# A two-layer encoder on one core: query units inside a gate's steps, unions ahead of weight sums, more low halves on GpSimd

## The chip, the cores and the metric

The kernel runs on one core of a Trainium2 chip, in one launch. The metric is the device time of one execution in microseconds (us), as the median of several runs. The core's engines are TensorE (PE in the profile; its weight loads are PEld), VectorE (DVE), ScalarE (ACT), GpSimd (POOL) and SyncE (SP, which here only issues transfers). Each runs its own list of instructions in the order in which the program wrote them, and waits for semaphores that the others raise.

## The reference, cut to what matters

Two layers, 512 tokens, 1024 channels. The change leaves every product as it is; what it moves belongs to the latent queries of branch A and to the gated feed-forward network.

```python
for l in range(DEPTH):
    h = rms_norm(x, attn_norm_g[l])
    c_q, c_kv, k_rope, gq, gk, gv, pool_in, gate_logits = split_columns(h @ w_in[l], IN_SIZES)
    o_mla = mla_branch(c_q, ...)      # q = rms_norm(c_q) @ w_uq: latent queries
    o_gqa = gqa_branch(gq, gk, gv, ...)
    o_pool = pool_branch(pool_in, ...)
    gates = sigmoid(gate_logits)
    merged = sum(gates[:, :, i] * (o_i @ w_branch_i[l]) for i in range(3))
    x = x + merged @ w_out[l]
    hf = rms_norm(x, ffn_norm_g[l])
    u = depthwise_conv(hf @ ffn_w_up[l], ffn_conv_w[l], ffn_conv_b[l])
    x = x + (silu(u[..., :D_FF]) * u[..., D_FF:]) @ ffn_w_down[l]
```

## The kernel before, in words

**Numbers and products.** All matrix products are float32 products in a reduced form (fp32r). Each operand is cut in two: a high half, which ScalarE rounds (`wh` of a weight, `HH`, `ah`, `qa`), and a low half, which is the rest (`wl`, `HL`, `al`, `qb`) and is a subtraction on VectorE or GpSimd. A product is three matmuls: high by high, low by high, high by low (`mm3`, line 491 through `mm`).

**Weights** come as one stream of pieces up to 512 columns wide, in the order of use. Pieces are packed into `raw` tiles up to 1024 wide, each filled by one transfer of SP; three such tiles rotate. `wnext` hands out the next piece and makes the halves of some pieces ahead: ScalarE writes `wh`, then `pick` chooses VectorE or GpSimd for `wl` by the planner's view of when each is free, unless `pool_only` is set, which puts them on GpSimd. Six `wh` and six `wl` buffers rotate.

**Pieces of seven.** Parts of the feed-forward products take seven block products for what needs eight (`products`, line 1911). For those a piece needs sums of its four blocks as well (`w_seven`): ScalarE copies one block into a PSUM tile (`ps_mi` or `ps_S`), VectorE makes the sums there (`both`, `third`, `fourth`), ScalarE rounds them (`hi`), VectorE makes their low half (`lo`). The plain blocks' low half (384 wide) is `rest`.

**The order** is not that of the source. `Clock` plans: every step of VectorE, ScalarE and GpSimd is put on a heap with a planned time and an assumed duration, and TensorE's own instructions advance the planned time; a step is written into its engine's list when the planned time passes it. `chain` runs steps one after the other, each after the planned end of the one before. Nothing of this is left at run time but the order of each engine's list and the semaphores.

**A layer's stages.** Input projections; grouped-query attention (GQA) with the gates and branch products of branch C as filling between its steps; latent attention (MLA) with the other branches as filling; the output product; the feed-forward network in two halves (`HALVES`: blocks 0 to 9, then 10 to 21). Each half first makes its up-products (`UPS`), then the down-products: for each of four pairs of output blocks (`m` = 0, 2, 4, 6) five or six calls of `products`, which fill four PSUM banks out of the six of the ring `acc`, `ST`, `AV` (two each), and then `unite`, which adds the four banks into the residual `XM`. The next pair starts on the two banks left and needs a third after 12 of its matmuls.

**In `unite`** ScalarE copies half of bank `b1` to `u`; VectorE adds `b0` to `XM` (and frees that bank), adds the other half of `b1` to the copy (and frees that bank), adds `b2` twice (and frees it), adds `u` to `b3`, and GpSimd and VectorE add the rest. In the first half `again` brings back `hsp` and `tsp`, which are cut into `HH`/`HL` and `tf` for the second half, low halves on GpSimd.

**Latent queries.** `make_q` makes one group's queries in four units of six matmuls, each into an `acc` bank that is free again when the unit's copy (`MQ`) is made. While such a unit list is active, one unit is put in on every even step of the gate that follows it; so the first unit stands ahead of the gate's first step, and its two weight pieces stand ahead of the gate's two.

Of the kernel before, what the change touches and what calls it, by code (L numbers as in the profile page):

```python
# [18 lines left out]
P = 128  # L19
T = 512  # L20
# [42 lines left out]
REST = 0.4  # L63
GAP = 2.0
PREP = (2, 5, 8, 11)
# [33 lines left out]
def _widths():  # L99

    r = [384] * KC + [T] * 8 + [T] * KC + [288] * 4 + [T] + [288] * 4
    for br in (2, 1, 0):
        late = []
        for k, _ in _order(br):
            if k in "nv":
                late = WIDTHS[k]
            else:
                r += WIDTHS[k][:1] + late + WIDTHS[k][1:]
                late = []
    return r + [T] * (2 * KC) + [T] * (4 * FC) + [T] * (2 * FC)  # L110
# [47 lines left out]
class Clock:  # L158
# [5 lines left out]
    def __init__(self):  # L164
        self.now, self.n, self.heap, self.busy = 0.0, 0, [], False
        self.fin, self.free, self.ready = 0.0, {}, {}
        self.source = self.last = None
        self.gives_way = {}
        self.locked = (0.0, 0.0)
# [50 lines left out]
    def chain(self, *steps, after=0.2):  # L220

        def go(n, source=None, since=None):
# [4 lines left out]
            if late and max(late) > self.now:  # L227
                self.at(max(late) - self.now, lambda: go(n))
                return
            eng, most = self.gives_way.get(fn, (None, 0.0))  # L230
# [83 lines left out]
def trunk(ctx: ExitStack, tc: tile.TileContext, x, w, prm, gb, cst, pad, out):  # L314
# [99 lines left out]
    def w_seven():  # L414
# [20 lines left out]
        def rest():  # L435
            e = pick(W_BIAS)
            e.tensor_tensor(los[0][:, :384], r[:, :384], f(his[0][:, :384]), ALU.subtract)
            done("wa", j)
            if j + 1 == len(pieces) or pieces[j + 1][0] > sl:
                at(max(0.0, ck.free[e.kind] - ck.now) + D_FREE, lambda: w_upto(sl + 1 + RAW))  # L440
# [14 lines left out]
        def lo():  # L455
            V.tensor_tensor(los[1], s[0], f(his[1]), ALU.subtract)
            done("w", j)

        chain(([("sums", j * L // len(pieces))] + ([("w", j - 2)] if seven[j - 2] else []), first), rest, after=0.0)
        chain(([("a21", j)], both), third, fourth, hi, lambda: done("wh", j), lo, after=0.01)  # L460
# [201 lines left out]
    def layer(l, sq, xsrc):  # L662
# [206 lines left out]
        def set_keys():  # L869
            for _, kb in KAB:  # L870
                G.memset(f(kb[64:P, :T]), 0.0)
                G.memset(f(kb[64:65 if "gqa" in PLAN else 96, :T]), 1.0)

        at(0.5, set_keys)

# [131 lines left out]
        def gates(br, okey, odst, mode):  # L1007
# [50 lines left out]
            for k, m in _order(br):  # L1058
                if k in mla_make:
                    extra, tick, when = mla_make[k](m), 0, k  # L1060
                    continue
                work = branch(m) if k == "b" else gate(m)
                more, first = True, tick
                while more:
                    n = tick - first
                    if extra and (tick % 2 == 0 if when == "q" else k == "g" and n in ((2, 6) if when == "n" else (3,))):
                        if next(extra, END) is END:
                            extra = None
                        yield
                    tick += 1  # L1070
                    more = next(work, END) is not END
                    yield
# [720 lines left out]
        def up_evac(c, part, acc, tag, scaled):  # L1793
# [77 lines left out]
            def turns():  # L1871
                eng = V if c + 1 == FC else G
                w0 = whole.pop(p)
                chain(diff(t3, 1, w0[:, 256:T], ALU.add), diff(t4, 0, t2, ALU.subtract), qfree,
                      *split(new[4][:, :T], new[5][:, :T], t34[:, :T], eng=eng), end(2), after=0.0)
                chain(*split(new[2][:, :T], new[3][:, :T], t12[:, :T], eng=eng), end(1), after=0.0)
# [10 lines left out]

        def products(right_, banks_, first, late=False):
            j = st["use"]
            his, los = (lambda z: (z[:2], z[2:]))(wnext())  # L1890
            (bh, bl), (ah, al), (ch, cl), (dh, dl), kb, ka, kc_, kd = right_
# [80 lines left out]
        def unite(m, banks_, then, early=False):  # L1972
# [10 lines left out]

            chain(lambda: A.activation(p1, b1[:, :256], AF.Copy), after=0.0)
            if early:
                chain(add(x0, x0, b0), add(u2, p1, b1[:, hi_]), add(x0[:, hi_], x0[:, hi_], b2[:, hi_]), add(x0, x0, u[:, :T]),
                      add(x1, x1, b2), add(b3[:, :256], u2, b3[:, :256]),
                      lambda: V.tensor_tensor(pair(x1), pair(x1), b3[:, None, :256].to_broadcast([P, 2, 256]), ALU.add), after=0.0)
                return
            chain(add(x0, x0, b0), lambda: free(t0), add(u2, p1, b1[:, hi_]), lambda: free(t1),  # L1990
                  add(x0[:, hi_], x0[:, hi_], b2[:, hi_]), add(x1, x1, b2), lambda: free(t2),
                  add(b3[:, :256], u2, b3[:, :256]),
                  add(x0, x0, u[:, :T], G), lambda: then and then(m),
# [28 lines left out]
        for c0, c1 in HALVES:  # L2022
            room[:] = spare
            for n_, (c, part) in enumerate(_ups(c0, c1)):
                if not c0 and n_ in PREP:
# [14 lines left out]
            for m in range(0, KC, 2):  # L2040
# [4 lines left out]
                for k in range(c0, c1 - 2 * PLAIN * end_, 2):  # L2045
                    products(right_of(k // 2), banks_, k == c0, m == 0 and k == c1 - 2)
                unite(m, banks_, finish if c1 == FC else None, end_)
# [80 lines left out]
def _pack_weights(i):  # L2128
    res = []
    for l in range(L):  # L2130
# [17 lines left out]
        for br in (2, 1, 0):  # L2148
            for k, m in _order(br):
# [7 lines left out]
                elif k == "q":  # L2157
                    res += [uq[kc * P:kc * P + P, m * 384:m * 384 + 384] for kc in range(2)]
                else:
# [98 lines left out]
```

## Time and profile before

| what | value |
|---|---|
| time, median of 3 runs | 1538.01 us (1537.58 to 1538.58) |
| the profiled execution's own time | 1538.08 us |
| its span | 1536.3 us |
| VectorE busy | 1206.2 us (79%) |
| ScalarE busy | 974.5 us (63%) |
| GpSimd busy | 1120.1 us (73%) |

In the profile a row of a timeline is: start, length, engine, line, operation, output tile <- input tiles, shape, how often in a row, and in brackets the idle time of the engine before it with what ended it. Matmuls overlap in time, so the length of a matmul row is longer than the step from its start to the next start. To see what a wait costs TensorE, take the distance of two starts and subtract the usual step.

### The profile page before, as it was taken

What the parts mean: (1) busy time and instruction counts of PE and PEld (TensorE: products, weight loads), DVE (VectorE), ACT (ScalarE), POOL (GpSimd) and SP (SyncE); (2) the same over time, 40 slices, a digit from 0 to 9 for tenths busy, and PEclk for the clock granted to TensorE, in tenths of its full rate; (3) what the DMA queues carried; (4) which work ended last, traced back from release to release, by engine and by line L of the source; (5) the groups of instructions that cost most, each with busy time, mean ns of one, the idle gap of its engine ahead of it and who ended that gap; (6) DMA issues with size and microseconds to landing.
All of it is one profiled execution on the core that took longest, in us unless ns stands there. A gap on an engine that the chain in (4) does not pass through costs nothing.

```text
span 1536.3 us, 25158 instructions
## 1 busy us (share of the span) xinstructions
PE 1519.1 (99%) x8390; PEld 1325.6 (86%) x8390; DVE 1206.2 (79%) x2386; ACT 974.5 (63%) x1961; POOL 1120.1 (73%) x1077
## 2 busy tenths in 40 slices
PE   9999999999999999999999999999999999999999
PEld 8888788788889899999998877888888899989998
DVE  6778889986578896778857788899865788867786
ACT  6557776664567665666654587766636677656763
POOL 4865986854689787675779659868547897967753
PEclk9999999999999999999999999999999999999999
DMA  6432234424344453333444322344243444533332
GB/s 219 117 111 78 76 92 139 130 91 132 105 140 147 148 176 106 94 103 109 133 129 136 102 70 76 112 134 130 79 151 96 141 148 138 182 107 100 95 121 84
DMA packets 91954, 183.56 MB, mean 119 GB/s; under 512 B 21936, under 2 KB 43696, under 8 KB 91824
## 3 DMA queue, kind: packets, MB, share of 16 engines
q1 hardware_dynamic: 91680, 181.94, 38.0%
q8 instruction: 66, 1.08, 0.3%
q14 instruction: 64, 0.52, 0.1%
q10 hardware_dynamic: 144, 0.01, 0.0%
HBM read 159.89 MB, written 22.02 MB: 118 GB/s over the span
## 4 chain that ended last, share of the span: by engine, by line
PE 75%; DVE 12%; ACT 6%; POOL 3%; issue 3%; DMA 1%; SPq 0%; ACTq 0%; DVEq 0%; POOLq 0%
PE ps_acc L491 24%; PE ps_AV L491 16%; PE ps_ST L1911 8%; PE ps_ST L491 8%; PE ps_acc L1911 7%; PE ps_AV L1911 6%; PE ps_S L491 2%; PE ps_mi L491 2%; ACT wh L272 2%; DVE nmt L290 1%; DVE wl L280 1%; DVE vt L284 1%; DVE XM L280 1%; DVE pl L280 1%; POOL qa L280 1%
## 5 line engine op out<-in xcount | busy, mean ns | idle before, releaser
L280 POOL TENSOR_TENSOR wl<-raw,wh 128x512 fp32r<-128x512 f32 (+3 forms) x487 | 579.7, 1200 | 306.3 <-ACT wh L272 267.0
L272 ACT ACTIVATE wh<-raw 128x512 fp32r<-128x512 f32 (+2 forms) x521 | 290.9, 577 | 21.1 <-PE ps_ST L491 11.3
L491 PE MATMUL ps_acc<-HH,wh 128*128 128x512 f32 x504 | 196.9, 391 | 0.1
L491 PE MATMUL ps_acc<-HL,wh 128*128 128x512 f32 x504 | 196.5, 390 | 0.0
L491 PE MATMUL ps_acc<-HH,wl 128*128 128x512 f32 x504 | 196.3, 389 | 0.0
L491 PEld LDWEIGHTS ps_acc<-HH,wl 128*128 128x128 f32 x504 | 94.6, 188 | 19.9
L491 PEld LDWEIGHTS ps_acc<-HH,wh 128*128 128x128 f32 x504 | 94.7, 188 | 19.7 <-DVE gt L280 0.6
L491 PEld LDWEIGHTS ps_acc<-HL,wh 128*128 128x128 f32 x504 | 94.7, 188 | 18.9
L491 PE MATMUL ps_AV<-HH,wh 128*128 128x512 f32 x248 | 96.7, 390 | 0.0
L491 PE MATMUL ps_AV<-HL,wh 128*128 128x512 f32 x248 | 96.6, 390 | 0.0
L491 PE MATMUL ps_AV<-HH,wl 128*128 128x512 f32 x248 | 96.5, 389 | 0.0
L272 ACT ACTIVATE wh<-ps_S 128x512 fp32r<-128x512 f32 x79 | 47.3, 598 | 49.2 <-DVE ps_S L280 37.8
L272 ACT ACTIVATE wh<-ps_mi 128x512 fp32r<-128x512 f32 x79 | 47.3, 598 | 46.5 <-DVE ps_mi L280 38.1
L280 DVE TENSOR_TENSOR wl<-ps_mi,wh 128x512 fp32r<-128x512 f32 x79 | 54.0, 684 | 12.2 <-ACT wh L272 10.6
L280 POOL TENSOR_TENSOR a<-a,cv 128x511 f32<-128x511 f32 x36 | 46.8, 1314 | 21.9 <-DVE a L284 21.9
L280 DVE TENSOR_TENSOR wl<-ps_S,wh 128x512 fp32r<-128x512 f32 x79 | 54.0, 684 | 10.6 <-ACT wh L272 9.7
L272 ACT ACTIVATE gt<-gt 128x512 f32<-128x512 f32 x48 | 30.2, 628 | 43.3 <-DVE gt L280 43.1
L1911 PE MATMUL ps_acc<-ah,wh 128*128 128x256 f32 x276 | 56.5, 283 | 0.0
L1911 PE MATMUL ps_ST<-ah,wh 128*128 128x256 f32 x294 | 55.5, 284 | 0.3 <-ACT wh L272 0.2
L290 DVE TENSOR_REDUCE nm<-ps_S 128x1 f32<-128x512 f32 x64 | 43.6, 682 | 15.1 <-PE ps_S L491 14.6
L272 ACT ACTIVATE ps_ST<-ps_ST 128x512 f32<-128x512 f32 x74 | 42.3, 583 | 20.1 <-PE ps_ST L491 12.4
L491 PEld LDWEIGHTS ps_AV<-HH,wl 128*128 128x128 f32 x248 | 46.6, 188 | 9.8
(560 smaller groups left out, 5201.2 us busy)
## 6 DMA issues: line engine op xcount, KB each, us to landing
raw<-w SPq DMA_DIRECT2D x228, 512.0 KB, 3.6
raw<-w SPq DMA_DIRECT2D x13, 384.0 KB, 3.1
XM<-x SPq DMA_DIRECT2D x16, 256.0 KB, 3.6
back<-hsp SPq DMA_DIRECT2D x16, 256.0 KB, 3.9
back<-tsp SPq DMA_DIRECT2D x16, 256.0 KB, 4.3
dtq<-tr SPq DMA_DIRECT2D x16, 192.0 KB, 1.9
dtk<-tr SPq DMA_DIRECT2D x16, 192.0 KB, 2.0
tf<-dtq SPq DMA_DIRECT2D x48, 64.0 KB, 2.1
```

Source lines behind the costliest of these rows:

```text
L272: return self.eng.activation(out, in_, func, **k)
L280: return self.eng.tensor_tensor(out, *a)
L284: return self.eng.scalar_tensor_tensor(out, *a)
L290: return self.eng.tensor_reduce(out, in_, *a, **k)
L491: PE.matmul(o, lhsT=lhsT, rhs=rhs, start=start, stop=stop)
L1911: PE.matmul(banks_[b][1][:, 256 * at_:256 * at_ + 256], lhsT=(his, his, los)[q][i][:, ws], rhs=right[n][q == 1], start=first and b not in ...
```

## The change

The edits are all of order and of the engine that does a step; the arithmetic is the same but for the place where the copy of `b1` is added.

- **Query units** (`_widths`, `_pack_weights`, `gates`): the two weight pieces of a query group now stand between the following gate's two pieces, and the units go in on odd steps, so the gate's first step comes first.
- **Union** (`unite`): ScalarE copies all 512 columns of `b1` and that bank is free; GpSimd, not VectorE, adds the two halves of the copy; VectorE's later step waits for that sum by the key `u2`.
- **Hold** (`HOLD`, `waits`, `pause`): `hi` and `lo` of a piece of seven, if planned between 0.65 us before and 0.15 us after the planned end of a pair's last products, are planned for the end of that stretch.
- **Low halves** (`ONLY`): in the first half of the feed-forward network `pool_only` is set, for `rest` of a piece of seven too.
- **Last turn**: in the second half the low half of `t34` of the last block goes to GpSimd as all others do.
- **GAP** 2.0 to 3.0: the cutting of what `again` brings is planned later.
- **set_keys**: four memsets of a layer go from GpSimd to VectorE, and are planned at 4.0 in place of 0.5.

```diff
-GAP = 2.0
+GAP = 3.0
+ONLY = True
+HOLD = (0.65, 0.15)
...
-            if k in "nv":
+            if k in "qnv":
                 late = WIDTHS[k]
             else:
                 r += WIDTHS[k][:1] + late + WIDTHS[k][1:]
...
-        self.gives_way = {}
+        self.gives_way, self.waits, self.pause = {}, set(), (0.0, 0.0)
...
+            if fn in self.waits and self.pause[0] <= self.now < self.pause[1] - 0.001:
+                self.at(self.pause[1] - self.now, lambda: go(n, source, since))
+                return
...
         def rest():
-            e = pick(W_BIAS)
+            e = G if pool_only[0] else pick(W_BIAS)
...
+        ck.waits.update((hi, lo))
...
         def set_keys():
             for _, kb in KAB:
-                G.memset(f(kb[64:P, :T]), 0.0)
-                G.memset(f(kb[64:65 if "gqa" in PLAN else 96, :T]), 1.0)
-
-        at(0.5, set_keys)
+                V.memset(f(kb[64:P, :T]), 0.0)
+                V.memset(f(kb[64:65 if "gqa" in PLAN else 96, :T]), 1.0)
+
+        at(4.0, set_keys)
...
-                    if extra and (tick % 2 == 0 if when == "q" else k == "g" and n in ((2, 6) if when == "n" else (3,))):
+                    if extra and (tick % 2 == 1 if when == "q" else k == "g" and n in ((2, 6) if when == "n" else (3,))):
...
-                      *split(new[4][:, :T], new[5][:, :T], t34[:, :T], eng=eng), end(2), after=0.0)
+                      *split(new[4][:, :T], new[5][:, :T], t34[:, :T], eng=G), end(2), after=0.0)
...
-        def products(right_, banks_, first, late=False):
+        def products(right_, banks_, first, late=False, end=False):
             j = st["use"]
+            if end:
+                ck.pause = (ck.now + 2.52 - HOLD[0], ck.now + 2.52 + HOLD[1])
...
-            chain(lambda: A.activation(p1, b1[:, :256], AF.Copy), after=0.0)
             if early:
+                chain(lambda: A.activation(p1, b1[:, :256], AF.Copy), after=0.0)
...
-            chain(add(x0, x0, b0), lambda: free(t0), add(u2, p1, b1[:, hi_]), lambda: free(t1),
+            chain(lambda: A.activation(u[:, :T], b1, AF.Copy), lambda: free(t1), add(u2, p1, u2, G), lambda k=c0: done("u2", l, m, k), after=0.0)
+            chain(add(x0, x0, b0), lambda: free(t0),
                   add(x0[:, hi_], x0[:, hi_], b2[:, hi_]), add(x1, x1, b2), lambda: free(t2),
-                  add(b3[:, :256], u2, b3[:, :256]),
+                  ([("u2", l, m, c0)], add(b3[:, :256], u2, b3[:, :256])),
...
+            pool_only[0] = ONLY and not c0
...
-                    products(right_of(k // 2), banks_, k == c0, m == 0 and k == c1 - 2)
+                    products(right_of(k // 2), banks_, k == c0, m == 0 and k == c1 - 2, k == c1 - 2)
...
                 elif k == "q":
-                    res += [uq[kc * P:kc * P + P, m * 384:m * 384 + 384] for kc in range(2)]
+                    late = [uq[kc * P:kc * P + P, m * 384:m * 384 + 384] for kc in range(2)]
```

Three places show how the lists of the engines change. First VectorE, at the union of the second pair in the first half of layer 0. `ps_mi` and `ps_S` are the tiles of weight sums, `wl` are low halves, `XM<-XM,ps_...` are the union's sums. Before:

```order
L280 TENSOR_TENSOR ps_mi_4839<-ps_mi_4839,raw_6321 128x256
L280 TENSOR_TENSOR wl_0_6447<-raw_6321,wh_0_6445 128x384
L280 TENSOR_TENSOR ps_mi_4839<-raw_6321,ps_mi_4839 128x128 x2
L280 TENSOR_TENSOR XM<-XM,ps_AV_6295 128x512
L280 TENSOR_TENSOR wl_1_6448<-ps_mi_4839,wh_1_6446 128x512
L280 TENSOR_TENSOR u_884_6480<-u_884_6480,ps_AV_6300 128x256
L280 TENSOR_TENSOR ps_S_4840<-ps_S_4840,raw_6321 128x256
L280 TENSOR_TENSOR XM<-XM,ps_acc_6314 128x256
```

After:

```order
L285 TENSOR_TENSOR ps_mi_4839<-ps_mi_4839,raw_6320 128x256
L285 TENSOR_TENSOR ps_mi_4839<-raw_6320,ps_mi_4839 128x128 x2
L285 TENSOR_TENSOR XM<-XM,ps_AV_6292 128x512
L285 TENSOR_TENSOR XM<-XM,ps_ST_6314 128x256
L285 TENSOR_TENSOR ps_S_4840<-ps_S_4840,raw_6320 128x256
L285 TENSOR_TENSOR XM<-XM,ps_ST_6314 128x512
L285 TENSOR_TENSOR ps_S_4840<-raw_6320,ps_S_4840 128x128
L285 TENSOR_TENSOR wl_1_6445<-ps_mi_4839,wh_1_6443 128x512
```

The low half of 384 columns is gone from VectorE's list, the sum into `u` too, and the weight sums' low half stands behind three of the union's sums.

GpSimd at the same place. `back` is what `again` brought, `tf` and `HL` its low halves, `XM<-XM,u` the union's part on GpSimd. Before:

```order
L280 TENSOR_TENSOR tf_6276<-back_6283,tf_6275 128x512
L280 TENSOR_TENSOR tf_6278<-back_6285,tf_6277 128x512
L280 TENSOR_TENSOR wl_0_6495<-raw_6321,wh_0_6493 128x384
L280 TENSOR_TENSOR wl_0_6536<-raw_6389,wh_0_6534 128x384
L280 TENSOR_TENSOR XM<-XM,u_884_6480 128x512
L280 TENSOR_TENSOR HL<-back_6485,HH 128x512
```

After:

```order
L285 TENSOR_TENSOR tf_6273<-back_6280,tf_6272 128x512
L285 TENSOR_TENSOR wl_0_6444<-raw_6320,wh_0_6442 128x384
L285 TENSOR_TENSOR u_884_6477<-u_884_6477 128x256
L285 TENSOR_TENSOR wl_0_6492<-raw_6320,wh_0_6490 128x384
L285 TENSOR_TENSOR tf_6275<-back_6282,tf_6274 128x512
L285 TENSOR_TENSOR XM<-XM,u_884_6477 128x512
L285 TENSOR_TENSOR wl_0_6537<-raw_6397,wh_0_6535 128x384
L285 TENSOR_TENSOR HL<-back_6482,HH 128x512
```

GpSimd has the 384 columns and the sum of `u` in addition, and the second `tf` stands behind them.

Third, GpSimd in the GQA stage of layer 0, where the other half of a pair's `qa` is made (`t_pair`, heads 4 and 5). `yt` and `y` are steps of the reciprocal root for the latent queries. Before:

```order
L280 TENSOR_TENSOR wl_1790<-raw_1541,wh_1789 128x512
L280 TENSOR_TENSOR yt_1723<-y_242_1722,ssm_1031 128x32
L280 TENSOR_TENSOR yt_1723<-yt_1723,y_242_1722 128x32
L294 TENSOR_SCALAR yt_1723<-yt_1723 128x32
L280 TENSOR_TENSOR y_242_1722<-yt_1723,y_242_1722 128x32
L280 TENSOR_TENSOR qa_1749<-tf_1585,qa_1749 64x512
```

After:

```order
L285 TENSOR_TENSOR wl_1723<-raw_1498,wh_1722 128x256
L285 TENSOR_TENSOR qa_1716<-tf_1583,qa_1716 64x512
L285 TENSOR_TENSOR qa_1719<-tf_1583,qa_1719 64x512
L315 MEMSET osum_1591 1x512 x2
L285 TENSOR_TENSOR oraw_1590<-oraw_1590,osum_1591 128x512
```

The four steps of the root now come later than `qa`, since the query units that feed them come later. Outside the two GQA stages TensorE's own list is the same in both but for the names of PSUM banks; in them, the query units stand at other places.

## The prediction

> **What bounds the kernel now.** I read the page first, then the list of who waited for whom on TensorE, then the timeline around each of its longer waits.
>
> ```profile
> span 1536.3 us, 25158 instructions
> PE 1519.1 (99%) x8390; PEld 1325.6 (86%) x8390; DVE 1206.2 (79%) x2386; ACT 974.5 (63%) x1961; POOL 1120.1 (73%) x1077
> ```
>
> TensorE is busy all the time and the change removes no matmul. So the whole prize is the time in which TensorE waits, and everything that the other engines save elsewhere is worth nothing. The page's 17 us of idle understate it, since matmul rows overlap; but the list tells for whom it waits:
>
> ```profile
> PE ps_AV L1911 <- DVE XM L280: 2.5, 2, 1.3
> PE ps_S L491 <- POOL qa L280: 2.0, 2, 1.0
> PE ps_ST L491 <- POOL qb L280: 1.4, 4, 0.4
> ...
> PE ps_ST L1911 <- DVE XM L280: 1.0, 2, 0.6
> ...
> PE ps_ST L1911 <- DVE wl L280: 0.6, 2, 0.4
> ```
>
> Nearly all come in twos: one a layer. Line 1911 is the feed-forward products, line 491 here the attention stage.
>
> **The first half's union.** The longest pair, 2.5 us, is where a new pair of blocks needs its third bank:
>
> ```profile
> 556.09 3.93 DVE L280 TENSOR_TENSOR wl<-raw,wh 128x384 fp32r<-128x384 f32 x1
> 560.47 0.68 DVE L280 TENSOR_TENSOR XM<-XM,ps_AV 128x512 f32<-128x512 f32 x1
> 557.05 2.55 POOL L280 TENSOR_TENSOR tf<-back,tf 128x512 fp32r<-128x512 f32 x2
> 559.42 0.40 PE L1911 MATMUL ps_acc<-sMK,wh 128*128 128x256 f32 x2
> 559.66 0.28 PE L1911 MATMUL ps_acc<-sMK,wl 128*128 128x256 f32 x1
> 561.20 0.51 PE L1911 MATMUL ps_AV<-sMQ,wh 128*128 128x256 f32 x2 [1.26 <-DVE XM L280]
> 561.90 0.28 PE L1911 MATMUL ps_AV<-sMK,wl 128*128 128x256 f32 x1
> 562.37 0.39 PE L1911 MATMUL ps_AV<-sMQ,wh 128*128 128x256 f32 x1 [0.20 <-DVE u L280]
> L272 ACT ACTIVATE wh<-ps_S 128x512 fp32r<-128x512 f32 x79 | 47.3, 598 | 49.2 <-DVE ps_S L280 37.8
> ```
>
> Two matmuls from 559.42 to 559.66 take 0.24, so one of 256 columns takes 0.12. From 559.66 to the next start at 561.20 are 1.54: 1.42 lost; 561.90 to 562.37 loses 0.35 more: 1.77 in all. The list's 2.5 for two waits, 1.3 the longest, says that layer 1 loses as much. The cause is one VectorE row: a low half of 384 columns, both inputs in SBUF, that runs from 556.09 to 560.02 while GpSimd works to 559.60. Behind it in VectorE's list stand the union's sums, which free the banks. The change puts this low half on GpSimd (in the first half all of them go there; three a layer move), and lets ScalarE free a bank by its own copy. Price of the new way: the third bank is wanted 12 x 0.12 = 1.44 after the new pair begins; a ScalarE copy of 512 columns from PSUM takes 0.60 (the fence's last row, from the page's groups) and VectorE's sum 0.68, side by side, so either is in time. I take the whole loss as gained: **-3.5** for two layers (-1.8 if half of it comes back).
>
> The Trainium skill, "SBUF — State Buffer", section "Who interferes with whom", says that a VectorE instruction with two SBUF inputs and a GpSimd instruction that reads SBUF shut each other out for a whole instruction. The trace agrees: the row ends 0.42 after GpSimd's run does. By that rule the new sum on GpSimd cannot be blocked by the union's sums on VectorE, which read PSUM; it changes no term.
>
> **The second half's begin and first union.**
>
> ```profile
> 719.94 0.28 PE L1911 MATMUL ps_ST<-ah,wl 128*128 128x256 f32 x1
> 720.44 0.50 PE L1911 MATMUL ps_ST<-ah,wh 128*128 128x256 f32 x2 [0.22 <-ACT wh L272]
> 721.16 0.39 PE L1911 MATMUL ps_ST<-ah,wl 128*128 128x256 f32 x1 [0.22 <-DVE wl L280]
> 724.14 0.28 PE L1911 MATMUL ps_acc<-sMK,wl 128*128 128x256 f32 x1
> 724.79 0.51 PE L1911 MATMUL ps_ST<-sMQ,wh 128*128 128x256 f32 x2 [0.37 <-DVE XM L280]
> 716.59 0.68 DVE L280 TENSOR_TENSOR ah<-ps_acc,ah 128x512 fp32r<-128x512 f32 x1
> 717.19 0.68 DVE L280 TENSOR_TENSOR ah<-t,ah 128x512 fp32r<-128x512 f32 x1
> 723.45 0.69 DVE L280 TENSOR_TENSOR wl<-ps_mi,wh 128x512 fp32r<-128x512 f32 x1 [0.74 <-ACT wh L272]
> 724.06 0.68 DVE L280 TENSOR_TENSOR XM<-XM,ps_ST 128x512 f32<-128x512 f32 x1
> ```
>
> At 720 weight sums come late: 0.50 - 0.12 = 0.38, then 0.72 - 0.24 = 0.48 lost. VectorE has three low halves of `ah` ahead of them; one moves to GpSimd, worth one step of 0.60 (716.59 to 717.19). So 0.6 of the 0.86 goes, in each layer: **-1.2** (0 to -2.2: layer 1 waits longer by the list). At 724, 0.65 - 0.12 = 0.53 and 0.10 behind it: the union's sum stands behind a weight's low half, begun 0.61 earlier. The hold turns the two round: 0.61 sooner, and ScalarE's copy frees a bank besides. The low half that now waits belongs to a product 2.52 (21 x 0.12) later, which hides it. By the list layer 1 loses 0.6 where layer 0 loses 0.37, so 0.9: **-1.5** (-0.7 to -1.5).
>
> **Attention.**
>
> ```profile
> 154.00 0.26 POOL L280 TENSOR_TENSOR yt<-y,ssm 128x32 f32<-128x32 f32 x1
> 155.31 1.81 POOL L280 TENSOR_TENSOR qa<-tf,qa 64x512 fp32r<-64x512 f32 x1
> 155.57 0.40 PE L491 MATMUL ps_acc<-HL,wh 128*128 128x512 f32 x1
> 155.80 0.39 PE L491 MATMUL ps_acc<-HH,wl 128*128 128x512 f32 x1
> 157.17 0.50 PE L491 MATMUL ps_S<-ka,qa 128*128 128x512 f32 x1 [0.98 <-POOL qa L280]
> 136.43 0.40 PE L491 MATMUL ps_acc<-HH,wl 128*128 128x512 f32 x1
> 137.50 0.44 PE L491 MATMUL ps_acc<-wh,cth 128*128 128x384 f32 x1 [0.67 <-DVE MQ L298]
> 95.54 0.33 PE L491 MATMUL ps_acc<-wh,cth 128*128 128x384 f32 x1
> 95.77 0.69 DVE L284 SCALAR_TENSOR_TENSOR XM<-gt,ps_acc 128x512 f32<-128x512 f32 x1
> ```
>
> A matmul of 512 columns takes 0.23. From 155.80 to 157.17 TensorE loses 1.14 on `qa`, and as the list has two such waits, 1.0 the longest, 1.14 in layer 1. GpSimd's `qa` stood behind four steps of a root (154.00 to 155.31: 1.31). These now stand behind it, as the query units that feed them come later; 1.31 sooner is more than 1.14: **-2.3** (-1.1 to -2.5: `qa` still follows a low half that waits for ScalarE). The second group's second query unit lost 1.07 - 0.23 = 0.84 in layer 0 for its bank, whose copy VectorE makes: six matmuls lay between (1.4). In the new list it is 13 (3.0): **-0.8** (0 to -0.8).
>
> Against that, the first query unit now takes the bank of the branch product just ahead, only three matmuls (0.68) after its last, where before a gate took it after six of 384 columns. The branch's product on VectorE ends at 96.46, TensorE would be there at 95.54 + 0.68 = 96.22, and resumes some 0.1 later: 0.3 a layer, **+0.6** (0 to +1.4). The other waits of this stage, above all the 1.4 for `qb`, are dealt anew with the order. Nothing in the rows says better or worse; GpSimd has more ahead of `qb` in places and less in others. I take **+1.0** (-2 to +4).
>
> **GpSimd's new work** in the first half's down-products:
>
> ```profile
> 546.00:586.00 40.00, 38.55 (x318) 38.05 (x317) 34.23 (x74) 25.84 (x61) 36.68 (x32) 1.00 0.52 172
> 562.23 1.99 POOL L280 TENSOR_TENSOR wl<-raw,wh 128x384 fp32r<-128x384 f32 x2 [2.62 <-ACT wh L272]
> 539.85 1.31 POOL L280 TENSOR_TENSOR ah<-t,ah 128x512 fp32r<-128x512 f32 x1 [0.93 <-ACT ah L272]
> L280 POOL TENSOR_TENSOR t<-a 128x256 f32<-128x256 f32 x22 | 16.4, 744 | 2.0 <-DVE a L280 2.0
> ```
>
> GpSimd is busy 36.68 of 40 there, and its one long gap (2.62) was the same VectorE row's doing. It gets three sums of `u` at 0.74, one low half of 384 columns at 1.0 (562.23: two in 1.99) and one of 512 at 1.3 (557.05: two in 2.55): 4.5, so 41.2 in 40 - 1.8 = 38.2. It falls 3.0 behind by the end of the stretch. Low halves are made two products ahead, 5.0, which covers it if it starts level (the 539.85 row). I take **+1.0** for two layers (0 to +6.0, the whole lag). The union's sum that needs `u` waits for GpSimd with VectorE's whole list behind it; VectorE has about 2.8 of other steps ahead of it (three sums at 0.6, one at 0.33 and two weight sums), against 0.74 and a low half of 1.0 on GpSimd, so it is covered at the first three unions.
>
> No cost for the rest: `kb`'s memsets and the replanned cuts lie where the list of waits shows none, the other twelve unions ended without a wait, the weights' bytes are the same, and in the second half GpSimd has room for the 0.74 and the 1.3 (724 to 769: no wait on it in the list).
>
> **Sum:** -3.5 - 1.2 - 1.5 - 2.3 - 0.8 + 0.6 + 1.0 + 1.0 = -6.7. The profiled execution took 1538.08 (the span and 1.8 around it), the median is 1538.01, so both give **1531.4**, 0.4% faster.
>
> **Rivals.** *Attention gives it back* (20%): the order planned with the same assumed durations has as many waits as before, each elsewhere. For it: the waits there ended on engines that ran late against the plan, and the plan's durations are unchanged. Then -2.3 and -0.8 are gone, and +0.6, +1.0 and +1.0 remain: 1538.1 - 6.2 + 2.6 = 1534.5. *No gain at the banks* (8%): another row of VectorE or a late ScalarE copy holds the unions, so the change does not do what it says. Then -3.5 and -1.5 fall out: 1536.4. Against it: the 3.93 row has no other cause in reach. *GpSimd becomes the bound in the first halves* (15%; slower than before): u's sum stands behind two more steps than I counted (a `tf` of 1.3 and a low half of 1.0), VectorE stands still at each of the eight unions there, and the next weight sums come late. A price of 1.3 a union (2.3 less about 1.0 of room) makes +10.4 in place of +1.0 and takes the -3.5: 1531.4 + 9.4 + 3.5 = 1544.3. It decides once GpSimd is over 3 us late at the first union. Against it: before, GpSimd is level with its work at 539.85, where it has waited 0.93 for ScalarE.
>
> The Trainium skill, "Perfetto Trace Analysis", section "Optimizing GPSIMD Operations", says to prefer other engines where possible, as GpSimd is generally slower. By that rule the last rival is the likely one, at its 1544.3. The trace so far bears it out in part: 0.74 for 256 columns on GpSimd against 0.68 for 512 on VectorE, yet off the path.
>
> **The numbers.** The forecast has 52%, attention better than I take it 5% (1527), the rivals 20, 8 and 15% in their order. A measurement of this kernel tells about 0.2% from no change, that is 3.1: faster means under 1534.9. The forecast is nearly all faster, the first rival a little over half, the second is no change, the third slower: faster 0.69, no change 0.15, slower 0.16. The forecast's own range is 1528 to 1534.5; the range takes in the first two rivals and the lower ends of the terms, 1527 to 1538.5.
>
> **What would show it.** In the changed profile TensorE's wait for `XM` at line 1911 is gone from the list, no VectorE row of a 384-column low half lasts over 3 us after 400 us, the wait of `ps_S` for `qa` is gone, and GpSimd is busy over 95% from 546 to 585 without TensorE waiting for its `wl`. A VectorE wait for `u` of over 1 us with TensorE waiting for weights just behind would prove the third rival. New waits of 1 us in the GQA stages would make the forecast wrong.

## The result, and the profile after

The changed kernel takes 1528.04 us (median of 6 runs, 1527.31 to 1529.66); the kernel before, measured beside it, 1537.67 (1537.11 to 1538.58). The ratio is 0.9937, with a 95% interval of 0.9925 to 0.9950: 9.6 us faster, where 6.7 were forecast. The profiled execution took 1529.66, the longest of the six; its span is 8.4 shorter than the span before.

The page of the changed kernel, its span and the busy time of the engines:

```profile
span 1527.9 us, 25186 instructions
PE 1515.6 (99%) x8390; PEld 1326.4 (87%) x8390; DVE 1190.6 (78%) x2368; ACT 979.2 (64%) x1963; POOL 1131.4 (74%) x1093
```

VectorE is busy 15.6 less and GpSimd 11.3 more, and neither number says anything of the 9.6. Who waited for whom on TensorE (total, times, longest) does:

```profile
PE ps_ST L497 <- POOL qb L285: 1.8, 2, 0.9
PE ps_S L497 <- POOL qa L285: 1.4, 3, 0.6
...
PE ps_ST L1919 <- DVE wl L285: 0.2, 1, 0.2
```

Line 1919 is the old 1911, line 497 the old 491. The 4.5 that the feed-forward products waited in the list of before (`XM` 2.5 and 1.0, `wl` 0.6, `u` 0.4) are down to 0.2; in attention the waits for `qa` and `qb` are still there, though at other places.

To size the stretches I take, for each matmul, the distance to the next start less the usual distance for its width (the median), and sum what is over. The whole loss is 27.6 before and 19.3 after; the difference of 8.3 is that of the spans, 8.4, within 0.1.

| TensorE's loss, us | before | after |
|---|---|---|
| start, 0 to 50 | 2.7 | 3.5 |
| attention with GQA, 50 to 250 and 850 to 1000 | 11.6 | 8.7 |
| latent attention, 250 to 400 and 1000 to 1150 | 5.0 | 5.5 |
| feed-forward, 450 to 800 and 1200 to 1550 | 8.1 | 1.4 |

So the feed-forward network gave 6.7 and attention 2.9. The start and latent attention came out 1.3 worse in this one execution, the longest of the six. Nothing is moved in TensorE's list there, and the profiles of the experiments below have from 2.7 to 3.3 and from 4.0 to 5.1 in these rows, so I take this for the scatter of single executions.

The timeline of the changed kernel at the first half's union, where before VectorE stood 3.93 us in one low half:

```profile
557.41 0.69 DVE L285 TENSOR_TENSOR XM<-XM,ps_AV 128x512 f32<-128x512 f32 x1 [0.55 <-PE ps_AV L1919]
557.53 0.60 ACT L277 ACTIVATE u<-ps_AV 128x512 f32<-128x512 f32 x1 [1.35 <-PE ps_AV L1919]
558.17 1.06 POOL L285 TENSOR_TENSOR wl<-raw,wh 128x384 fp32r<-128x384 f32 x1
558.89 0.28 PE L1919 MATMUL ps_acc<-sMK,wl 128*128 128x256 f32 x1
559.01 0.40 PE L1919 MATMUL ps_AV<-sMQ,wh 128*128 128x256 f32 x2
```

VectorE waits for TensorE here, not TensorE for VectorE: the sum of 557.41 and ScalarE's copy of 557.53 begin as soon as the products are done and both are over by 558.13. TensorE goes from the new pair's second bank (558.89) to the third (559.01) in 0.12, one usual step.

The busy times in the stretch of the first half's down-products (TensorE, its loads, VectorE, ScalarE, GpSimd):

```profile
546.00:586.00 40.00, 40.00 (x323) 39.44 (x323) 28.95 (x69) 26.94 (x62) 40.00 (x38) 1.00 0.56 182
```

And one row of the timeline, at the last union of the first half in layer 0:

```profile
586.75 0.43 DVE L285 TENSOR_TENSOR ps_ST<-u,ps_ST 128x256 f32<-128x256 f32 x1 [2.33 <-POOL u L285]
```

GpSimd has no gap at all, and VectorE did wait 2.33 for GpSimd's sum of `u`. TensorE lost nothing by it: its list of waits shows no weight there.

Last, where attention still waits, in layer 0:

```profile
177.21 1.28 POOL L285 TENSOR_TENSOR wl<-raw,wh 128x512 fp32r<-128x512 f32 x1
178.57 1.28 POOL L285 TENSOR_TENSOR qa<-tf,qa 64x512 fp32r<-64x512 f32 x1
178.94 0.39 PE L497 MATMUL ps_acc<-HH,wl 128*128 128x512 f32 x1
179.90 0.51 PE L497 MATMUL ps_S<-ka,qa 128*128 128x512 f32 x1 [0.57 <-POOL qa L285]
192.88 1.29 POOL L285 TENSOR_TENSOR MQ<-MQ,tabm 128x512 f32<-128x512 f32 x1
194.25 1.18 POOL L285 TENSOR_TENSOR qb<-nmt,unit 32x128 fp32r<-32x128 f32 x2
194.18 0.39 PE L497 MATMUL ps_ST<-qa,ka 128*128 128x512 f32 x1
195.48 0.50 PE L497 MATMUL ps_ST<-qb,kb 128*128 128x512 f32 x1 [0.91 <-POOL qb L285]
96.76 0.39 PE L497 MATMUL ps_acc<-HH,wl 128*128 128x512 f32 x1
97.34 0.41 PE L497 MATMUL ps_acc<-wh,cth 128*128 128x384 f32 x1 [0.19 <-DVE XM L289]
```

At 178.94 TensorE loses 0.96 - 0.23 = 0.73 on the first `qa` of the last pair of heads, which stands behind a low half (the pair's second `qa` is made from 181.80 on); at 194.18 it loses 1.30 - 0.23 = 1.07 on `qb`, behind a step of the queries' rotation (`MQ`). Both are in layer 1 too. At 96.76 the first query unit loses 0.35 on the branch's bank.

### The profile page after: what moved, and what is told of

It reads as the page before. It is cut to its first block, busy times and chain, and to the rows that moved or that the text cites. A ratio compares the mean times of both kernels' runs of the same rounds, so it can differ in the third digit from the quotient of the medians.

```text
span 1527.9 us, 25186 instructions
## 1 busy us (share of the span) xinstructions
PE 1515.6 (99%) x8390; PEld 1326.4 (87%) x8390; DVE 1190.6 (78%) x2368; ACT 979.2 (64%) x1963; POOL 1131.4 (74%) x1093
## 4 chain that ended last, share of the span: by engine, by line
PE 86%; DVE 6%; ACT 3%; POOL 2%; issue 1%; DMA 1%; SPq 0%; POOLq 0%; ACTq 0%; DVEq 0%
PE ps_acc L497 29%; PE ps_AV L497 17%; PE ps_ST L1919 9%; PE ps_ST L497 9%; PE ps_acc L1919 8%; PE ps_AV L1919 7%; PE ps_S L497 2%; PE ps_mi L497 2%; PE ps_ST L1460 1%; DVE XM L285 1%; POOL MQ L285 1%; DVE nmt L295 1%; DVE pl L285 1%; DVE vt L289 1%; ACT wh L277 1%
## 5 line engine op out<-in xcount | busy, mean ns | idle before, releaser
L285 POOL TENSOR_TENSOR wl<-raw,wh 128x512 fp32r<-128x512 f32 (+3 forms) x494 | 585.9, 1195 | 285.9 <-ACT wh L277 249.3
L285 DVE TENSOR_TENSOR wl<-ps_mi,wh 128x512 fp32r<-128x512 f32 x79 | 54.1, 685 | 11.3 <-ACT wh L277 10.0
L1919 PE MATMUL ps_ST<-ah,wh 128*128 128x256 f32 x298 | 59.9, 284 | 0.1
L497 PEld LDWEIGHTS ps_AV<-HH,wh 128*128 128x128 f32 x248 | 46.6, 188 | 9.8 <-ACT wh L277 0.5
```

The source lines that it names most:

```text
L285: return self.eng.tensor_tensor(out, *a)
L497: PE.matmul(o, lhsT=lhsT, rhs=rhs, start=start, stop=stop)
L1919: PE.matmul(banks_[b][1][:, 256 * at_:256 * at_ + 256], lhsT=(his, his, los)[q][i][:, ws], rhs=right[n][q == 1], start=first and b not in ...
```

## The experiments

All times are medians; "before" is the kernel before, measured beside the row on the same chip. The rows come from several chips, whose "before" differ by up to 0.9, so a difference between two rows of the first column is good to about 1 us at best. The last two columns are TensorE's loss in the one profile of each kernel, summed as above over the feed-forward and the GQA stretches. They are sharper than the times, whose intervals are about 2 us to each side: the ten kernels that share the change's plan of the query units have 8.6 to 8.9 in attention.

| kernel | us | before | ratio (95%) | feed-forward | attention |
|---|---|---|---|---|---|
| before | 1537.67 | | | 8.1 | 11.6 |
| the change | 1528.04 | 1537.67 | 0.9937 (0.9925 to 0.9950) | 1.4 | 8.7 |
| no_hold | 1530.75 | 1537.41 | 0.9957 (0.9943 to 0.9970) | 4.1 | 8.9 |
| no_only | 1528.39 | 1537.41 | 0.9939 (0.9927 to 0.9952) | 1.3 | 8.9 |
| old_union | 1527.82 | 1537.41 | 0.9939 (0.9927 to 0.9951) | 1.4 | 8.9 |
| old_q | 1531.64 | 1537.41 | 0.9962 (0.9950 to 0.9975) | 2.1 | 11.9 |
| only_alone | 1535.51 | 1538.03 | 0.9983 (0.9974 to 0.9992) | 5.3 | 11.6 |
| q_alone | 1534.57 | 1538.03 | 0.9977 (0.9968 to 0.9986) | 8.0 | 8.7 |
| rest_back | 1530.62 | 1538.03 | 0.9954 (0.9941 to 0.9966) | 4.5 | 8.6 |
| t34_back | 1529.07 | 1538.28 | 0.9940 (0.9927 to 0.9952) | 2.6 | 8.8 |
| no_hold_old_union | 1531.29 | 1538.28 | 0.9952 (0.9939 to 0.9964) | 4.6 | 8.7 |
| last_pair | 1532.05 | 1538.28 | 0.9959 (0.9945 to 0.9972) | 1.6 | 12.1 |
| u2_x2 | 1536.58 | 1538.17 | 0.9993 (0.9984 to 1.0002) | 9.9 | 8.7 |
| u2_x3 | 1538.04 | 1538.03 | 0.9999 (0.9990 to 1.0008) | 10.9 | 8.7 |

### The query units: q_alone and old_q

q_alone is the kernel before with the three edits on the query units; old_q is the change with them undone, as the diff shows.

```diff
-            if k in "qnv":
+            if k in "nv":
-                    if extra and (tick % 2 == 1 if when == "q" else k == "g" and n in ((2, 6) if when == "n" else (3,))):
+                    if extra and (tick % 2 == 0 if when == "q" else k == "g" and n in ((2, 6) if when == "n" else (3,))):
-                    late = [uq[kc * P:kc * P + P, m * 384:m * 384 + 384] for kc in range(2)]
+                    res += [uq[kc * P:kc * P + P, m * 384:m * 384 + 384] for kc in range(2)]
```

> The kernel before with the query units alone moved (packing and odd steps). Theory: attention gains the 3.0 that the two traces differ by: 1534.7. Rival: the plan of this stage depends on the rest of the change (the memsets on VectorE), and by itself gives the waits back elsewhere: -1.0 to +1.0, 1537.7.

> The change with the query weights packed ahead and the units on even steps, as before. Theory from the two traces (TensorE's lost time from 50 to 250 us is 2.2 less after, from 850 to 1000 us 0.8 less): +3.0, 1531.0, with the waits for qa of 1.1 back in both layers. Rival: the attention waits are re-dealt by luck and any replanning of the stage comes out the same: within 1.0 of 1528.0.

Alone the edits gave 3.5, and undoing them cost 3.6 (1531.64 against 1528.04). The profiles say 2.9 and 3.2 in the GQA stretches; old_q loses 0.7 more in the feed-forward network besides, in short waits near 722 and 1275 whose cause was not followed. So this part is worth about 3 us with the rest of the change and without it, and the two parts of the change add up. It is the same plan in both: q_alone's waits in this stage are those of the change, at the same places and of the same size (0.77 and 1.04 where the change has 0.73 and 1.07).

### The low halves of the first half: only_alone and no_only

only_alone adds one rule to the kernel before (`pool_only[0] = not c0` at the head of a half, and `e = G if pool_only[0] else pick(W_BIAS)` in `rest`); no_only sets `ONLY = False` in the change. Of the three rows that only_alone takes off VectorE in a layer, the third (at 583.4 in layer 0) has 512 columns, not 384 as its expectation says.

> The kernel before with one edit: in the first half all low halves go to GpSimd (three a layer move, the rows of 384 columns at 524.3, 556.1 and 583.4 and their counterparts). Theory: the 3.93 row alone held the first half's union; -3.5 to -3.9, 1533.9, no wait for XM at the feed-forward products in the first half. Rival: VectorE's sums still free the third bank too late without ScalarE's whole copy and the hold: -1.5, 1536.2, and a shorter wait for XM stays.

> The change with the planner choosing the engine of every low half again. It puts one low half of 384 columns a layer, ahead of the first down-products of the first half, back on VectorE, and no other. Theory: no union stands behind it, so nothing is lost: 1528.0 (0 to +0.5), and the two rows of about 4 us at 556 and 1319 stay away. Rival: each 384-column row on VectorE beside a busy GpSimd costs TensorE what the one at 556 did: +1.8 a layer, 1531.6.

In only_alone the waits at both unions of the first half, 1.98 and 1.96 by the distances, are gone, with the union as it was and without the hold. VectorE's rows there read:

```profile
557.83 0.69 DVE L280 TENSOR_TENSOR wl<-ps_mi,wh 128x512 fp32r<-128x512 f32 x1 [0.74 <-ACT wh L272]
558.53 0.69 DVE L280 TENSOR_TENSOR XM<-XM,ps_AV 128x512 f32<-128x512 f32 x1
```

The weight sums' low half still stands ahead of the union's sum; at 0.69 it is short enough. So the low halves on VectorE, of which the 3.93 row is the one that stands there, were the whole cause. The kernel gained only 2.5, since layer 1 lost 0.8 anew at the second half's up-products (see rest_back) and 0.4 at its begin of down-products. no_only put one 384-column row back on VectorE:

```profile
522.52 1.15 DVE L285 TENSOR_TENSOR wl<-raw,wh 128x384 fp32r<-128x384 f32 x1
```

Nothing waits behind it and the time is the same: the rival, a price for each such row, falls. The run shows more than it was made for: the row of 556 stays off VectorE without `ONLY`, as the planner, with the other edits in place, gives that low half to GpSimd by itself. So inside the change `ONLY` is worth nothing that was measured; which of the other edits turns the planner's choice was not run.

### The union and the hold: old_union, no_hold, no_hold_old_union

old_union takes the first form of `unite` back into the change, no_hold sets `HOLD = (0.0, 0.0)`, the third does both.

```diff
-            chain(lambda: A.activation(u[:, :T], b1, AF.Copy), lambda: free(t1), add(u2, p1, u2, G), lambda k=c0: done("u2", l, m, k), after=0.0)
-            chain(add(x0, x0, b0), lambda: free(t0),
+            chain(lambda: A.activation(p1, b1[:, :256], AF.Copy), after=0.0)
+            chain(add(x0, x0, b0), lambda: free(t0), add(u2, p1, b1[:, hi_]), lambda: free(t1),
...
-                  ([("u2", l, m, c0)], add(b3[:, :256], u2, b3[:, :256])),
+                  add(b3[:, :256], u2, b3[:, :256]),
```

> The change with the union as before: ScalarE copies half of the bank, VectorE adds the other half, GpSimd has no u sum. Theory: the low halves are what held the first half's union, and they stay on GpSimd, so only the small wait for u returns: +0.4 to +0.8, 1528.6. Rival: ScalarE's whole copy is what frees the third bank in time: the 1.8 to 2.0 a layer come back, 1531.8.

> The change without the hold (both of its times 0). Theory: the second half's first union stands behind a weight's low half again, so TensorE's wait there comes back, 0.6 to 0.9 a layer: +1.5, 1529.5 us, and the list of waits shows XM at the feed-forward products of the second half. Rival: ScalarE's copy already frees the third bank in time, so that the hold is worth nothing: 1528.0.

> The change with neither the hold nor the new union. The hold alone undone cost 2.7, the new union alone undone nothing. Theory: without the hold ScalarE's copy stands behind the rounding of a weight sum (0.66 late at 734 and at 750), so the new union needs the hold; without both, VectorE's sum stands behind a weight's low half as before, 0.5 to 0.9 at the second half's first union: +1.5, 1529.5. Rival: the 2.7 came of replanned weight sums in general, whatever the union: +2.7, 1530.7. Third: with the low halves off VectorE the old union needs no hold: 1528.0.

The new union is worth nothing once the hold is there. The hold is worth 2.7 with the new union and, by the third run, 3.5 with the old one (1531.29 against old_union's 1527.82; 2.6 when each is taken against its own "before"); by TensorE's loss in the feed-forward network 2.7 and 3.2. What it prevents differs. Without the hold, with the new union:

```profile
734.12 0.60 ACT L277 ACTIVATE wh<-ps_mi 128x512 fp32r<-128x512 f32 x1 [1.23 <-DVE ps_mi L285]
734.62 0.59 ACT L277 ACTIVATE u<-ps_ST 128x512 f32<-128x512 f32 x1
734.48 0.28 PE L1919 MATMUL ps_AV<-sMK,wl 128*128 128x256 f32 x1
735.26 0.50 PE L1919 MATMUL ps_ST<-sMQ,wh 128*128 128x256 f32 x2 [0.50 <-ACT u L277]
```

ScalarE's copy, which is to free the bank, stands behind the rounding of a weight sum, and TensorE waits for the copy: 0.66 here and 0.64 at the next union, both in layer 0; the rest of the 2.7 is in smaller steps. The wait for `XM` that the expectation named did not come back. Without the hold, with the old union:

```profile
719.11 0.69 DVE L285 TENSOR_TENSOR wl<-ps_mi,wh 128x512 fp32r<-128x512 f32 x1 [0.75 <-ACT wh L277]
719.72 0.68 DVE L285 TENSOR_TENSOR XM<-XM,ps_ST 128x512 f32<-128x512 f32 x1
719.55 0.28 PE L1919 MATMUL ps_acc<-sMK,wl 128*128 128x256 f32 x1
720.45 0.50 PE L1919 MATMUL ps_ST<-sMQ,wh 128*128 128x256 f32 x2 [0.62 <-DVE XM L285]
```

This is the wait of the prediction, XM behind a low half. My 1.5 for it was right for the first union, 0.78 a layer here; but later unions of layer 1 lose 0.47 twice in the same way, which did not happen in the kernel before. The total is thus nearer to the rival's 1530.7 than to my 1529.5, though not by the rival's reason: what is lost is lost on `XM`. old_union's rival (ScalarE's whole copy is what frees the bank in time), no_hold's rival (the copy alone suffices) and the third possibility of no_hold_old_union all fall.

### The small edits: rest_back and t34_back

rest_back sets `GAP = 2.0`, puts the memsets back on GpSimd at 0.5 and the last `t34` back on VectorE; t34_back does only the last.

> The change with the three small edits undone: GAP 2.0, the memsets on GpSimd at 0.5, the last low half of t34 by the old choice. Theory: none of them lies on a wait: 1528.0, within 1.0. Rival: the later cutting of what comes back keeps GpSimd clear at the first half's unions, and without it u comes late there: +2 or more, 1530.

> The change with the low half of t34 of the last block back at the old choice (VectorE); GAP and the memsets stay changed. It splits the 2.6 that undoing the three small edits cost. Theory: this edit is the second half's begin, priced at 1.2 for two layers: 1529.2, with TensorE losing 0.4 and 0.4 near 716 and as much near 1473. The rest of the 2.6, about 1.4, is then GAP's, at the second half's up-products. Rival: all of it is GAP's: 1528.0.

The first expectation called all three edits free, though the prediction had priced that of `t34` at 1.2. t34_back loses 1.2 by the distances, as priced (1.0 by the medians, 0.4 when each is taken against its own "before", neither clear of the noise):

```profile
716.76 0.28 PE L1919 MATMUL ps_acc<-ah,wl 128*128 128x256 f32 x1
717.22 0.50 PE L1919 MATMUL ps_ST<-ah,wh 128*128 128x256 f32 x2 [0.18 <-ACT wh L277]
717.95 0.39 PE L1919 MATMUL ps_ST<-ah,wl 128*128 128x256 f32 x1 [0.23 <-DVE wl L285]
```

The other 1.9 of rest_back's 3.1 (by the distances; 2.6 by the medians) lie in the feed-forward network: 0.3 a layer around 558 and 1317, 0.9 at layer 1's second up-products, and 0.3 near 1468. Around 558 the trace shows the way:

```profile
555.50 2.60 POOL L285 TENSOR_TENSOR tf<-back,tf 128x512 fp32r<-128x512 f32 x2
558.02 1.05 POOL L285 TENSOR_TENSOR wl<-raw,wh 128x384 fp32r<-128x384 f32 x1
559.12 0.39 PE L1919 MATMUL ps_ST<-sMQ,wl 128*128 128x256 f32 x1
```

Two `tf` stand in GpSimd's list ahead of a low half that ends at 559.07, and TensorE takes it 0.24 late. In the change one `tf` stands there. The cutting of `tf` is what GAP plans.

At the second up-products a low half on VectorE takes three times as long as in the change. First rest_back:

```profile
1368.44 1.30 POOL L285 TENSOR_TENSOR sMQ<-t,sMQ 128x512 fp32r<-128x512 f32 x1
1368.51 1.66 DVE L285 TENSOR_TENSOR wl<-raw,wh 128x384 fp32r<-128x384 f32 x1
1429.74 0.39 PE L1919 MATMUL ps_AV<-HH,wl 128*128 128x256 f32 x1 [0.30 <-DVE wl L285]
```

In the change the first two of these read:

```profile
1369.26 1.64 POOL L285 TENSOR_TENSOR sMQ<-t,sMQ 128x512 fp32r<-128x512 f32 x1
1369.19 0.55 DVE L285 TENSOR_TENSOR wl<-raw,wh 128x384 fp32r<-128x384 f32 x1
```

The two steps are the same, only the order of their starts is not. In rest_back GpSimd begins 0.07 earlier and VectorE's step is the long one; in the change VectorE begins 0.07 earlier and GpSimd's step is. VectorE stays behind from there on: from 1370 to 1387 its rows stand 0.4 later in rest_back than in the change, while TensorE's stand 0.8 earlier, and at 1387 TensorE begins to lose. only_alone has the bad order too (1372.65 and 1372.70, 1.64 long); the kernel before has the good one (1376.37, 0.55 long). So this cost hangs on 0.1 us of order, which no edit aims at. What moves VectorE's start by that much was not followed. The memsets belong to attention, whose loss is the same in rest_back, so GAP is the likelier of the two edits behind the 1.9; but they were not run apart, and for the up-products nothing beyond the place speaks for it.

### More work on GpSimd: u2_x3 and u2_x2

GpSimd's sum of `u` is made two or three times at each union of the first half (`*[add(u2, p1, u2, G)] * (2 * (not c0))` behind the first, or once). `u` is then no longer the sum that the reference asks for; only the time is of use.

> The change with GpSimd's sum of u made three times at each union of the first half (two more of 0.74, so 1.5 later and 12 us more GpSimd work in all; u is then not the reference's). Theory: VectorE has 2.8 of other steps before it wants u, GpSimd 0.74 and at most one low half of 1.0, so 1.5 more uses the room up without passing it by much: +0 to +2, 1529. The rival by which GpSimd is the bound in the first halves: each of the eight unions is late by the whole 1.5: +12, 1540.

> The change with GpSimd's sum of u made twice at each union of the first half (3.0 more of GpSimd work a layer; u is then not the reference's). Three times made 5.9 more a layer and cost 10.0 in all, 5.0 a layer, so by one pool of spare time that is used up first the room is 0.9 a layer. Theory: then 3.0 more costs 2.1 a layer, +4, 1532. Rival: the room is per union (VectorE's other steps ahead of it), where 0.74 fits: 0 to +1, 1528.5, and the cost of the three-times version came of single weights that crossed a threshold.

Both cost far more than I expected, u2_x2 8.5 and u2_x3 10.0 more than the change, and not in proportion to the work: neither room, one pool or per union, describes it. The timeline of u2_x2 shows a row that may be why:

```profile
583.34 10.05 DVE L285 TENSOR_TENSOR wl<-raw,wh 128x512 fp32r<-128x512 f32 x1
582.93 2.54 POOL L285 TENSOR_TENSOR wl<-raw,wh 128x512 fp32r<-128x512 f32 x2
...
591.55 1.28 POOL L285 TENSOR_TENSOR XM<-XM,u 128x512 f32<-128x512 f32 x1
597.94 0.74 POOL L285 TENSOR_TENSOR sMK<-a,sMK 128x256 fp32r<-128x256 f32 x1 [5.11 <-ACT sMK L277]
```

The planner, which sees GpSimd full, gave one low half of 512 columns to VectorE, at the very end of the first half. GpSimd then worked without a gap until 592.83, and VectorE's step ended at 593.39: 10.05 us for a step that takes 0.65 where VectorE gets in between two GpSimd steps (at 775.8 in the change), with all of VectorE's list behind it. It takes 9.3 in layer 1, and 8.6 in both layers of u2_x3. About 3 us a layer are lost in the 50 us that follow; late low halves near 553 and 1316 cost 0.3 to 1.1 a layer besides. It is the same fault as the 3.93 row of the kernel before, 2.6 times as long. That the 3 us come of this row, and not of GpSimd's lag as such, is argued from the order in time; a version with this low half kept on GpSimd was not run.

### A version that might beat both: last_pair

In the change, for head 6, the two rows of `qb`, and for the last pair the second `qa`, go from GpSimd to VectorE.

```diff
-                        (G if h else V).tensor_tensor(qa[other, :T], tp[own], f(qa[own, :T]), ALU.subtract)
+                        (V if h in (0, 6) and (i or not h) else G).tensor_tensor(qa[other, :T], tp[own], f(qa[own, :T]), ALU.subtract)
...
-                            G.tensor_tensor(o[:, :, g], n, bc(f(unit[32 * g:32 * g + 32, 0:1].unsqueeze(2)), [32, 4, 32]), ALU.mult)
+                            (V if h == 6 else G).tensor_tensor(o[:, :, g], n, bc(f(unit[32 * g:32 * g + 32, 0:1].unsqueeze(2)), [32, 4, 32]), ALU.mult)
```

> A version that may beat both: the change, and for the last pair of heads the two steps of GpSimd for which TensorE waits longest in attention, the second low part of qa (0.73 lost a layer) and the two rows of qb for head 6 (1.08 a layer), go to VectorE. VectorE stands idle 1.4 and 1.7 there. Theory: both waits go and nothing else moves: -3.6, 1524.4. Rival: TensorE's own list is replanned at eight places by it and the waits turn up elsewhere: within 1.0 of 1528.0.

It is 4.0 slower than the change (3.4 by TensorE's loss in attention). Its list of waits on TensorE begins:

```profile
PE ps_acc L497 <- DVE gt L285: 1.6, 4, 0.6
PE ps_S L497 <- POOL qa L285: 1.4, 3, 0.6
PE ps_S L497 <- DVE nm L295: 1.4, 2, 0.7
PE ps_ST L497 <- DVE qb L285: 1.2, 2, 0.6
```

The waits for `qb` are shorter by a third, those for `qa` are as long as in the change:

```profile
178.15 1.28 POOL L285 TENSOR_TENSOR qa<-tf,qa 64x512 fp32r<-64x512 f32 x1
179.48 0.50 PE L497 MATMUL ps_S<-ka,qa 128*128 128x512 f32 x1 [0.57 <-POOL qa L285]
180.63 1.22 DVE L285 TENSOR_TENSOR qa<-tf,qa 64x512 fp32r<-64x512 f32 x1
183.23 0.51 PE L497 MATMUL ps_S<-ka,qa 128*128 128x512 f32 x1 [0.69 <-DVE nm L295]
```

The expectation named the wrong step. The `qa` that TensorE waits for is the pair's first, at 178.15, and the edit moved the second, at 180.63; so the wait of 0.74 stayed. The moved step stands in VectorE's list ahead of the maxima (`nm`) that free the bank of the scores, and these come late: 0.85 lost at 183.23 where the change loses 0.14. VectorE is waited for elsewhere too (`gt`), and TensorE's own list was dealt anew in part, so more was given back than won. A version with the first `qa` on VectorE was not run. old_union ties with the change; no version faster than the change was found.

## Why the prediction was right, and where its sizes were off

The direction, the range and the mechanism held: the loss lay in TensorE's waits, and the banks and query units gave it back. The forecast of -6.7 was 2.9 short of -9.6, and 1528.04 lies at the very edge of its own range of 1528 to 1534.5, near the 1527 that was given 5% (attention better than taken). Term by term, by the distances of starts:

| term, two layers | forecast | measured |
|---|---|---|
| first half's union | -3.5 | -3.9 |
| second half's begin | -1.2 | -1.1 |
| second half's first union | -1.5 | -1.5 |
| `qa` at 155.8 and 918.2 | -2.3 | -2.5 |
| second query unit's bank | -0.8 | -0.4 |
| first query unit on the branch's bank | +0.6 | +0.7 |
| the other GQA waits, dealt anew | +1.0 | -0.8 |
| GpSimd's new work | +1.0 | 0 |
| sum | -6.7 | -9.5 |

The sum leaves out the 1.3 by which the start and latent attention came out worse in the profiled execution. Two terms came out larger than forecast for one reason, the first half's union by 0.4 and `qa` by 0.2: the step behind each wait is some 0.10 longer as well (the two matmuls at 561.20 take 0.34 to the next start at 561.54, not 0.24), and there the prediction counted the wait alone.

- **First half's union.** Right, and shown by only_alone to be the doing of the low halves on VectorE. The argument that "either is in time" (ScalarE's copy or VectorE's sum) was right too: old_union does without the copy. The new union is not needed. Nor, inside the change, is the rule by which the prediction moves the row: in no_only the row stays away without it.
- **Second half's begin** was right, with t34_back behind it.
- **Second half's first union** was right in size; the cause named, the sum behind a weight's low half, is shown by no_hold_old_union. What the prediction said of ScalarE's copy ("frees a bank besides") was only half true: without the hold the copy itself comes late.
- **Attention.** The waits named went or came nearly as sized, but for the second query unit's bank, which keeps half of its loss in two waits of 0.18. What was off in the sum are the two terms that no row carried, this one and the next: the waits dealt anew were taken at +1.0, as nothing spoke either way, and came out at -0.8. New ones did appear (0.73 for `qa` and 1.07 for `qb` in each layer), so that the sign "the wait of `ps_S` for `qa` is gone" was wrong and that of new waits of 1 us came true; but more old ones went. That they did is luck as far as is known: q_alone and the change have the same plan in this stage, so that they agree says nothing of another plan, and last_pair, which deals the stage anew in part, gives 3.4 back.
- **GpSimd's new work** was priced at +1.0, a sixth of its lag of 3.0 a layer. Nothing was paid, though GpSimd was busy for 40.00 of 40 and VectorE did wait 2.33 for `u`. The cover that the prediction named, low halves made two products ahead, held: TensorE waits for no `wl` there.
- **"No cost for the rest"** was right in the sum and wrong in its reason: the small edits beside `t34` are not idle. rest_back, without them, loses 1.9 more; for the part around 558 the trace points at GAP, for the up-products the cost hangs on which of two steps begins first.
- **The rivals.** Attention did not give it back and the banks gained in full. GpSimd did not become the bound; but half of its sign came, VectorE's wait of over 1 us for `u`, without TensorE waiting behind it, and a plan with 3.0 more of its work a layer is 8.5 slower. As far as the traces show, that comes by another way than the rival said, through a VectorE step shut out, not through `u`.

## What to carry to other kernels

Look for a step that takes several times its usual length before you count busy shares: where VectorE reads two inputs from SBUF while GpSimd works without a pause, the step can last until GpSimd pauses, and the cure is to take that step off VectorE, not to make either engine less busy. Undo each edit of a bundle alone and in pairs: here the hold was worth 3 us, and the new union and the rule for the low halves, each undone alone, nothing. Before you move a step because it is waited for, make sure by its start and end that it is the one. In a stage whose order is planned, moving it deals other waits anew, and only a run tells how.

## What the runs showed of the hardware

That VectorE can be shut out for so long was not expected. The Trainium skill, "SBUF — State Buffer", section "Who interferes with whom", calls the port pair that VectorE's second SBUF input shares with GpSimd's reads an exclusive lock, and says that issue order decides who blocks. The trace agrees where the two begin 0.07 apart: the one that begins second takes longer, VectorE 1.66 in place of 0.55 (rest_back, 1368.51) or GpSimd 1.64 in place of 1.30 (the change, 1369.26).

But VectorE also waited for a whole run of GpSimd instructions, nine from 582.93 to 592.83 in u2_x2, and came in only when the run ended (10.05 us; 3.93 in the kernel before, whose run of GpSimd ended at 559.60 and whose step at 560.02). It was not always so. In the kernel before, GpSimd worked without a pause from 578.70 to 592.45, and VectorE's row in the middle of it was much shorter:

```profile
583.42 1.89 DVE L280 TENSOR_TENSOR wl<-raw,wh 128x512 fp32r<-128x512 f32 x1 [1.86 <-ACT wh L272]
584.72 1.75 POOL L280 TENSOR_TENSOR wl<-raw,wh 128x512 fp32r<-128x512 f32 x1
```

Here VectorE came in behind the GpSimd instruction that ended at 584.76, and the next one on GpSimd took 1.75 in place of 1.30. So VectorE does get in between two GpSimd instructions at times; what decides it stays open.
